# The first pass of a two-layer hybrid decoder: dot products of the conditioning, their order on two engines, and where small parameter work stands

## The chip, the cores and the metric

The kernel runs on one core of a Trainium2 chip. A core has TensorE (PE, matrix products; PEld loads its weights), VectorE (DVE), ScalarE (ACT), GpSimd (POOL) and SyncE (SP, which here issues most transfers). The metric is device time in microseconds of one execution; a lower time is better.

## What is computed

The reference is a decoder trunk of two layers on 512 tokens of width 1024, in float32. What matters here is the start of a layer:

```python
for l in range(DEPTH):
    cond = jax.nn.silu(c) @ w_ada[l] + b_ada[l]
    shift, scale, gate_raw = jnp.split(cond, 3, axis=-1)
    h = x * (1.0 + scale[:, None]) + shift[:, None]
    proj = h @ w_in[l]          # 49 column tiles of 128: HGRN2, RWKV-7, merge gates
    ...                         # two token mixers on proj, merged by sigmoid gates
    x = layer_norm(DN_ALPHA * x + (1.0 + gate_raw[:, None]) * out, ln_g[l], ln_b[l])
```

The vector `c` (1024 numbers) sets, through a dot product with each column of `w_ada`, one shift and one scale for each of the 1024 channels of `h`. Nothing of the projection can start on a slice of `h` before the shift and the scale of its 128 channels are there. `lower_bounds`, a softmax over the two layers of a small parameter, enters the forget gate of HGRN2.

## The kernel before, in words

Channels lie on the 128 partitions and tokens on the free axis, so `h` is eight slices ("columns" below, `kt` 0 to 7) of 128 channels x 512 tokens. Each product is made of three: operands are cut into a rounded part (hi) and a remainder (lo), and hi x hi, hi x lo and lo x hi are added in PSUM.

**Start.** One row of `c` is loaded (L149), a product with a row of ones (L168) spreads it over all partitions in two halves of 512, and `c_rows` (L173) makes silu of it with a tanh on ScalarE and one operation on VectorE for each half. `NWARM` = 5 products on a mask (L928) keep TensorE busy meanwhile. VectorE also prepares small parameters of both layers (L209 to L239: scaled copies, and the softmax with two exponentials on ScalarE).

**First pass** (L876 to L951). For each column `kt`, `first_load` loads 128 x 512 of `x` and two tiles of `w_ada` (128 x 1024 each, 512 KB), and `ada_col` makes the shift (`dvsh`) and the scale (`dvsc`): two half dots of 512 and an addition for each, by L309. `first_h` makes the slice of `h` on ScalarE (`u`, L124), rounds it (`A`, L122, ScalarE) and takes the remainder on VectorE (`A`, L127). Seven column tiles of `w_in` (`first`, L863) are then multiplied with the slice, so that a column gives 21 products (L949 to L951) into seven PSUM tiles, which stay open over all eight columns. The weights come in 28 pieces of 128 x 256 (`unit_loads`); `unit_splits` rounds each on ScalarE (L122) and takes its remainder on GpSimd (L127); a piece serves two columns. The table `ORD` says behind which column which load is issued: a number below 8 is the load of that column, 8 the masks, and 11, 20 and 21 the second, third and fourth seven pieces of weights.

**After it.** The seven PSUM tiles feed the heads of layer 0: `hg_f` (tanh on ScalarE, then two operations on VectorE with `dvh` and `dvlbm`, the softmax's results), `hg_q`, and so on. Head by head, the chains of the mixers are woven with further projections (L268 to L273).

**What sets the order.** The program is written as one stream; a scheduler places the instructions of each engine in an order of its own, within data dependences, buffers and what `issue_after` demands. Each engine then works strictly in its order. SyncE issues transfers in order too, and waits where the target is still being read.

Of the kernel before, what the change touches and what calls it, by code (L numbers as in the profile page):

```python
# [19 lines left out]
WAZ = (1, 1, 1, 1, 1, 1, 1, 1)  # L20
WAB = (1, 1, 1, 1, 1, 1, 1, 1, 0)
NWARM = 5
ORD = ((11, 2), (3, 20), (4,), (5, 6), (21,7), (8,), (), ())

WHZ = (0, 16, 5, 6, 7, 7, 8, 6, 4, 4)
WHS = (0, 14, 5, 6, 7, 8, 9, 8, 6, 6)
# [57 lines left out]
def body(ctx, tc, d):  # L84
    nc = tc.nc
    V, A, G, PE = nc.vector, nc.scalar, nc.gpsimd, nc.tensor
# [18 lines left out]
    def u(shape=(128, 512), dt=F32):  # L105
        return st("u", list(shape), dt)
# [10 lines left out]
    def cst(name, shape, dt=F32):  # L117
        return cp.tile(list(shape), dt, name=name)

    def act(out, in_, f, scale=1.0, bias=0.0):  # L120
        if f == AF.Copy:
            A.activation(out, in_, f, scale=scale)  # L122
# [21 lines left out]
    mm = PE.matmul  # L144
    PK = (A.copy, V.tensor_copy)


    crow = st("G", [1, 1024])
    nc.sync.dma_start(crow, d["c"].rearrange("(a k) -> a k", a=1))  # L149
    prm = cst("prm", (128, NPRM))  # L150
    nc.scalar.dma_start(prm, d["prm"])
    cc = cst("cc", (128, NCONST))
# [11 lines left out]
    ones = u((128, 128))  # L164
    G.memset(ones, 1.0)
    craw = [ps("rw"), ps("rw")]
    for h in range(2):
        cmm = mm(craw[h], ones[0:1], crow[:, h * 512:(h + 1) * 512], start=True, stop=True)  # L168
    mbd = cst("mbd", (128, 4, 128))
    silc = []  # L170

    def c_rows(craw):

        silc[:] = [mbd.rearrange("p a b -> p (a b)"), st("W", [128, 512])]
# [4 lines left out]
    c_rows(craw)  # L179
    ident = cc[:, NC_ID:NC_ID + 128]  # L180
    bonesr = cst("bonesr", (128, 128), F32R)
    for i in range(2):
# [11 lines left out]
    cs = cst("cs", (128, 8))  # L194
# [4 lines left out]
    def P(n, l, i=None, w=None):  # L199
        o = PO[n, l]  # L200
        if i is not None:
            return prm[:, o + i:o + i + 1]
        return prm[:, o:o + w]

    dv = [dict() for _ in range(L)]
    for l in range(L):
        for n, w in (("omm", 17), ("omka", 4), ("h1", 4), ("h1n", 4), ("lbm", 4), ("kkh", 4), ("sc1", 8), ("sh", 8),
                     ("ga", 8)):
            dv[l][n] = cst(f"dv{n}{l}", (128, w))  # L209
        ts(V, dv[l]["omm"], P("mu", l, w=17), -1.0, 1.0, ALU.mult, ALU.add)  # L210
        V.tensor_scalar_mul(dv[l]["kkh"], P("kk", l, w=4), -0.5)
        ts(V, dv[l]["omka"], P("ka", l, w=4), -0.5, 1.0, ALU.mult, ALU.add)

        for n in ("w0", "a0", "ka", "v0")[:4 if l else 3]:
            V.tensor_scalar_mul(P(n, l, w=4), P(n, l, w=4), 0.5)
        V.tensor_scalar_add(P("bsc", l, w=16), P("bsc", l, w=16), 1.0)


    lbm = cst("lbm", (128, 4))
    lbe = [cst(f"lbe{l}", (128, 4)) for l in range(L)]  # L220
    lb = cst("lb", (128, 4))
    lbt = cst("lbt", (128, 4))
    tt(V, lbm, P("lbr", 0, w=4), P("lbr", 1, w=4), ALU.max)
    for l in range(L):
        tt(V, lbe[l], P("lbr", l, w=4), lbm, ALU.subtract)
        act(lbe[l], lbe[l], AF.Exp)
    tt(V, lbt, lbe[0], lbe[1], ALU.add)
    V.reciprocal(lbt, lbt)
    for l in range(L):
        mul(V, lbe[l], lbe[l], lbt)  # L230
    for l in range(L):
        if l == 0:
            tt(V, lb, lbe[0], lbe[0], ALU.subtract)
        else:
            tt(V, lb, lbe[0], lbe[1], ALU.add)
            tt(V, lb, lb, lbe[0], ALU.subtract)
        ts(V, dv[l]["h1"], lb, -0.5, 0.5, ALU.mult, ALU.add)
        V.tensor_scalar_mul(dv[l]["h1n"], dv[l]["h1"], -1.0)
        V.tensor_scalar_max(dv[l]["lbm"], lb, 1e-30)  # L239


    piece = [512]

    def split(raw, hi, lo, e=None):

        act(hi, raw, AF.Copy)
        for i in range(0, raw.shape[-1], piece[0]):
            x = slice(i, min(i + piece[0], raw.shape[-1]))
            tt(e or G, lo[:, x], raw[:, x], hi[:, x].bitcast(F32), ALU.subtract)

    def wunit(src, th="wh", tl="wl"):
        raw = st("raw", [128, 512])
# [49 lines left out]
    def ada_col(l, n, k, w, run=True):  # L302

        o = dv[l][("sh", "sc1", "ga")[n]][:, k:k + 1]
        init = P(("bsh", "bsc", "bga")[n], l, k)
        part = st("sm", [128, 2])

        def half(h):
            V.tensor_tensor_reduce(out=w[h], in0=w[h], in1=silc[h], scale=0.5, scalar=0.0 if h else init, op0=ALU.mult,  # L309
                                   op1=ALU.add, accum_out=part[:, h:h + 1])  # L310
            if h:
                tt(V, o, part[:, 0:1], part[:, 1:2], ALU.add)
        if run:
# [566 lines left out]
    xin = []  # L880

    def first_load(kt):
        if kt % 2 == 0:
            xin.append(st("t4" if kt < 6 else "G", [128, 2, 512]))
        if kt:
            nc.sync.dma_start(xin[kt // 2][:, kt % 2], d["xt"][kt])
        hs = []
        for n in range(2):
            w = wada[kt % 2][:, (kt // 2 % 2 * 2 + n) * 1024:(kt // 2 % 2 * 2 + n) * 1024 + 1024]
            nc.sync.dma_start(w, d["w_ada"][0, n, kt])  # L890
            hs.append(ada_col(0, n, kt, (w[:, 0:512], w[:, 512:1024]), kt > 0))
        if kt == 0:
            nc.sync.dma_start(xin[0][:, 0], d["xt"][0])
            for f in hs:
                for h in range(2):
                    f(h)

    def first_h(kt):
        hx = u()
        sc, sh = dv[0]["sc1"][:, kt:kt + 1], dv[0]["sh"][:, kt:kt + 1]  # L900
        if kt == 0:
            ts(V, hx, xin[0][:, 0], sc, sh, ALU.mult, ALU.add)
        else:
# [97 lines left out]
    for l in range(L):  # L1001
# [409 lines left out]
```

## Time and profile before

| what | value |
|---|---|
| time, median of 3 runs | 977.59 us (976.17 to 984.16) |
| profiled execution | 974.99 us, span 973.1 us |
| PE busy | 931.4 us, 96% of the span |
| DVE busy | 736.9 us, 76% |
| POOL busy | 584.5 us, 60% |
| ACT busy | 455.8 us, 47% |
| mean granted TensorE clock | 0.99 of full speed |

The span is the time from the first to the last instruction of the profiled execution; 1.9 us lie around it. A matrix unit that is busy 96% of the span still has stretches in which it waits; the table does not tell where they lie, and stretches, waits and single instructions are read for that.

### The profile page before, as it was taken

The numbers are of one execution on the slowest core, as the hardware profiler recorded it, in microseconds if no ns is written. First come the engines' busy times: TensorE is split into PE (matmuls) and PEld (weight loads), VectorE is DVE, ScalarE is ACT, GpSimd is POOL, SyncE is SP. The second block draws the span as 40 slices with busy tenths as digits, with TensorE's granted clock in tenths as the row PEclk, the third lists the DMA queues.
The fourth block names the chain that finished last, engine by engine and source line by source line (L and its number), as shares of the span: only waits on it lengthen the run. The fifth ranks groups of instructions, "written<-read, shape, count | busy, mean of one in ns | idle before, by whom it ended". The sixth has DMA issues, their size and how long they took to land.

```text
span 973.1 us, 16762 instructions
## 1 busy us (share of the span) xinstructions
PE 931.4 (96%) x6132; PEld 753.2 (77%) x6132; DVE 736.9 (76%) x1277; ACT 455.8 (47%) x924; POOL 584.5 (60%) x568
## 2 busy tenths in 40 slices
PE   7888899999999999999999999999999999999996
PEld 3666688888877777888888778888888777778786
DVE  7878986769995667588876686767799676747777
ACT  3356455556334334543355655556633433453421
POOL 5466666566454666867546577667745466674435
PEclk9999999999998999999999999999999999999998
DMA  8815322323332231565642123222233323355422
GB/s 320 325 49 168 119 88 66 97 74 91 93 106 86 88 120 44 161 203 188 196 135 65 56 87 87 66 87 78 75 98 89 117 89 108 101 163 172 120 77 86
DMA packets 61748, 112.83 MB, mean 116 GB/s; under 512 B 6865, under 2 KB 11361, under 8 KB 61666
## 3 DMA queue, kind: packets, MB, share of 16 engines
q1 hardware_dynamic: 57778, 105.12, 34.8%
q10 hardware_dynamic: 3888, 6.64, 2.1%
q8 instruction: 48, 0.79, 0.3%
q14 instruction: 34, 0.28, 0.1%
HBM read 106.49 MB, written 5.25 MB: 115 GB/s over the span
## 4 chain that ended last, share of the span: by engine, by line
PE 61%; DVE 23%; DMA 3%; issue 2%; ACT 2%; POOL 1%; DVEq 0%; ACTq 0%; POOLq 0%
PE ppj L273 13%; PE ppj L268 13%; PE ppj L269 12%; DVE t L127 5%; DVE t L543 3%; DVE ar L546 2%; PE prw L599 2%; DVE t L535 2%; DMA raw<-in_w_br 2%; PE ppj L1211 2%; PE ppj L1212 2%; PE ppj L1210 2%; DVE u L127 1%; PE prw L618 1%; DVE hl L127 1%
## 5 line engine op out<-in xcount | busy, mean ns | idle before, releaser
L127 POOL TENSOR_TENSOR wl<-raw,wh 128x256 fp32r<-128x256 f32 (+1 forms) x321 | 349.5, 1103 | 256.8 <-ACT wh L122 136.8
L122 ACT ACTIVATE wh<-raw 128x512 fp32r<-128x512 f32 (+1 forms) x233 | 145.1, 625 | 172.7 <-PE ppj L269 103.3
L268 PE MATMUL ppj<-B,wh 128*128 128x512 f32 x432 | 173.6, 402 | 0.1
L269 PE MATMUL ppj<-B,wh 128*128 128x512 f32 x432 | 170.9, 396 | 0.0
L268 PE MATMUL ppj<-A,wh 128*128 128x512 f32 x400 | 161.8, 405 | 1.6 <-ACT wh L122 1.6
L269 PE MATMUL ppj<-A,wh 128*128 128x512 f32 x400 | 159.1, 398 | 0.0
L273 PE MATMUL ppj<-B,wl 128*128 128x512 f32 x432 | 123.7, 397 | 0.0
L273 PE MATMUL ppj<-A,wl 128*128 128x512 f32 x400 | 116.2, 402 | 0.0
L268 PEld LDWEIGHTS ppj<-B,wh 128*128 128x128 f32 x432 | 81.2, 188 | 16.8 <-ACT wh L122 0.5
L273 PEld LDWEIGHTS ppj<-B,wl 128*128 128x128 f32 x432 | 79.8, 188 | 16.8 <-POOL wl L127 0.2
L269 PEld LDWEIGHTS ppj<-B,wh 128*128 128x128 f32 x432 | 81.4, 188 | 14.7
L268 PEld LDWEIGHTS ppj<-A,wh 128*128 128x128 f32 x400 | 75.7, 189 | 18.5 <-ACT wh L122 3.1
L273 PEld LDWEIGHTS ppj<-A,wl 128*128 128x128 f32 x400 | 74.6, 190 | 15.6
L269 PEld LDWEIGHTS ppj<-A,wh 128*128 128x128 f32 x400 | 75.6, 189 | 13.4
L127 DVE TENSOR_TENSOR t<-t,t 128x144 f32<-128x144 f32 (+29 forms) x62 | 44.3, 715 | 2.1
L127 POOL TENSOR_TENSOR hl<-hl,u 128x256 f32<-128x256 f32 x40 | 32.1, 803 | 20.2 <-DVE u L787 9.6
L136 DVE SCALAR_TENSOR_TENSOR pr<-ppj,prm,pr 128x511 f32<-128x511 f32 x22 | 16.4, 748 | 29.6 <-ACT pr L124 29.6
L127 DVE TENSOR_TENSOR hl<-hl,u 128x256 f32<-128x256 f32 x64 | 32.5, 527 | 2.6 <-ACT u L805 1.3
L127 DVE TENSOR_TENSOR W<-prw,d 64x256 f32<-64x256 f32 x32 | 13.5, 422 | 20.0 <-PE prw L623 19.2
L517 ACT COPY X<-prw 64x128 f32<-64x128 f32 x64 | 16.8, 262 | 24.2 <-PE prw L513 23.5
L543 DVE TENSOR_REDUCE t<-t 128x4 f32<-128x4 f32 (+30 forms) x62 | 26.4, 425 | 2.1
L127 POOL TENSOR_TENSOR gm<-mbd,gam 64x256 f32<-64x256 f32 x24 | 18.9, 787 | 15.1 <-DVE mbd L127 12.3
(488 smaller groups left out, 1992.8 us busy)
## 6 DMA issues: line engine op xcount, KB each, us to landing
raw<-in_w_in SPq DMA_DIRECT2D x182, 256.0 KB, 2.6
B<-in_w_ada SPq DMA_DIRECT2D x16, 512.0 KB, 6.5
z<-in_w_ada SPq DMA_DIRECT2D x32, 256.0 KB, 3.1
u<-in_w_ada SPq DMA_DIRECT2D x32, 256.0 KB, 3.5
raw<-in_w_br SPq DMA_DIRECT2D x32, 256.0 KB, 2.7
raw<-in_w_out SPq DMA_DIRECT2D x32, 256.0 KB, 2.7
u<-in_x SPq DMA_DIRECT2D x8, 256.0 KB, 4.3
o<-in_w_in SPq DMA_DIRECT2D x14, 128.0 KB, 4.4
```

The lines of the kernel that those rows point to most:

```text
L122: A.activation(out, in_, f, scale=scale)
L127: return e.tensor_tensor(o, a, b, op=op)
L268: yield mm(o, w, xh, start=half == 0 and k == 0, stop=False)
L269: yield mm(o, w, xl, start=False, stop=False)
L273: yield mm(o, w, xh, start=False, stop=half == n - 1 and k == 3)
L535: V.transpose(Tin[qs].rearrange("p t s -> p s t"), ax[qs, :, cs_].rearrange("p h s -> p s h"))
L543: V.tensor_reduce(blk(R, t, [32, j]), pv, axis=AX.X, op=ALU.add)
L546: V.transpose(ax[qs, :, cs_].rearrange("p h t -> p t h"), R[qs].rearrange("p j t -> p t j"))
L599: mm(pg[h][:, p * 128:(p + 1) * 128], BK[p][hs, ch], ZR[p][hs, ch], start=p == 0, stop=p == 3)
L1210: yield mm(p2[:, q], mg[j][:, 0, o], wo[j][0][:, q], start=j == 0, stop=False)
L1211: yield mm(p2[:, q], mg[j][:, 0, o], wo[j][1][:, q], start=False, stop=False)
L1212: yield mm(p2[:, q], mg[j][:, 1, o], wo[j][0][:, q], start=False, stop=j == 7)
```

## The change

Five things change.

1. `c` is loaded in two halves onto partitions 0 and 64, and the two spreading products stand on different row groups of TensorE; silu of `c` lies in one tile of 1024 (`silc0`) instead of two of 512.
2. A shift or a scale is one dot of 1024 with the bias as its start value and the result written at once; the additions go.
3. VectorE's order in the first pass is written out (`queued`, the list `chain`): scale dot of a column, shift dot of the next, remainder of this one. ScalarE's too (`units`). GpSimd's remainders of the first weights stand behind the first scale (`shown`).
4. The small parameters, but for the biases, are prepared behind the last slice (`of_parameters`), with the two exponentials.
5. `ORD` loads column 4 ahead of the third seven pieces of weights (20).

```diff
-ORD = ((11, 2), (3, 20), (4,), (5, 6), (21,7), (8,), (), ())
+ORD = ((11, 2), (3, 4), (20,), (5, 6), (21, 7), (8,), (), ())
...
-    crow = st("G", [1, 1024])
-    nc.sync.dma_start(crow, d["c"].rearrange("(a k) -> a k", a=1))
+    crow = st("G", [128, 512])
+    for h in range(2):
+        nc.sync.dma_start(crow[64 * h:64 * h + 1], d["c"][h * 512:(h + 1) * 512].rearrange("(a k) -> a k", a=1))
...
-        cmm = mm(craw[h], ones[0:1], crow[:, h * 512:(h + 1) * 512], start=True, stop=True)
+        cmm = mm(craw[h], ones[64 * h:64 * h + 1], crow[64 * h:64 * h + 1], start=True, stop=True)
...
+    silc0 = st("G", [128, 1024])
+    c_rows(craw, [silc0[:, h * 512:(h + 1) * 512] for h in range(2)])
...
+    def of_parameters():
+        ...
+        tt(V, lbm, P("lbr", 0, w=4), P("lbr", 1, w=4), ALU.max)
+        for l in range(L):
+            tt(V, lbe[l], P("lbr", l, w=4), lbm, ALU.subtract)
+            act(lbe[l], lbe[l], AF.Exp)
+        ...
...
-            hs.append(ada_col(0, n, kt, (w[:, 0:512], w[:, 512:1024]), kt > 0))
+            ws[kt].append(w)
...
+    def queued(f, q=None):
+
+        q = chain if q is None else q
+        with ExitStack() as es:
+            if q:
+                es.enter_context(tc.issue_after(q[-1].ins))
+            q.append(f())
+
+    def first_col(kt, n):
+        w = ws[kt][n]
+        o = dv[0][("sh", "sc1")[n]][:, kt:kt + 1]
+        queued(lambda: V.tensor_tensor_reduce(out=w, in0=w, in1=silc0, scale=0.5, scalar=P(("bsh", "bsc")[n], 0, kt), op0=ALU.mult,
+                                              op1=ALU.add, accum_out=o))
 
     def first_h(kt):
+
         hx = u()
         sc, sh = dv[0]["sc1"][:, kt:kt + 1], dv[0]["sh"][:, kt:kt + 1]
+        first_col(kt, 1)
         if kt == 0:
-            ts(V, hx, xin[0][:, 0], sc, sh, ALU.mult, ALU.add)
+            queued(lambda: V.tensor_scalar(hx, xin[0][:, 0], sc, sh, op0=ALU.mult, op1=ALU.add))
         else:
-            act(hx, xin[kt // 2][:, kt % 2], AF.Identity, scale=sc, bias=sh)
-        hilo(hx, hT[kt], V)
+            queued(lambda: act(hx, xin[kt // 2][:, kt % 2], AF.Identity, scale=sc, bias=sh), units)
+        rounded = A.activation(hT[kt][:, 0], hx, AF.Copy)
+        if kt:
+            units.append(rounded)
+        low = lambda: queued(lambda: tt(V, hT[kt][:, 1], hx, hT[kt][:, 0].bitcast(F32), ALU.subtract))
+        if kt == 0:
+            low()
+        if kt < KT - 1:
+            first_col(kt + 1, 0)
+        if kt:
+            low()
+        return rounded
...
-            split(fr[i][:, w], fw[i][0][:, w], fw[i][1][:, w])
+            queued(lambda: split(fr[i][:, w], fw[i][0][:, w], fw[i][1][:, w]), units)
...
+    first_load(1)
+    first_col(0, 0)
     first_h(0)
-    unit_splits(0, 0)
-    first_load(1)
+
+    shown = G.tensor_copy(cs[:, 7:8], dv[0]["sc1"][:, 0:1])
+    with tc.issue_after(shown.ins):
+        unit_splits(0, 0)
...
-            first_h(kt + 1)
+            rounded = first_h(kt + 1)
+            if kt == 6:
+                with tc.issue_after(rounded.ins), tc.issue_after(chain[-1].ins):
+                    of_parameters()
```

On VectorE, behind the remainder of column 0 (`A_166`), the order before was the following (`B` holds the tiles of `w_ada`, `mbd` and `W` the halves of silu of `c`, `sm` the two partial sums, `dvsh` and `dvsc` shift and scale):

```order
L127 TENSOR_TENSOR A_166<-u_199,A_166 128x512
L309 ISA B_165,sm_233<-B_165,mbd,prm 128x512
...
L309 ISA B_165,sm_233<-B_165,W_77 128x512
...
L127 TENSOR_TENSOR dvsh_100<-sm_233 128x1
L309 ISA B_165,sm_238<-B_165,mbd,prm 128x512
...
L309 ISA B_165,sm_238<-B_165,W_77 128x512
...
L127 TENSOR_TENSOR dvsc_99<-sm_238 128x1
L127 TENSOR_TENSOR A_166<-u_261,A_166 128x512
```

In the change, from the same place (the left out rows, in both, read the accumulator):

```order
L127 TENSOR_TENSOR A_131<-u_160,A_131 128x512
L912 ISA B_130,dvsh_101<-B_130,G_78,prm 128x1024
...
L912 ISA B_130,dvsc_100<-B_130,G_78,prm 128x1024
...
L912 ISA B_129,dvsh_101<-B_129,G_78,prm 128x1024
...
L127 TENSOR_TENSOR A_131<-u_206,A_131 128x512
L912 ISA B_129,dvsc_100<-B_129,G_78,prm 128x1024
```

The remainder of column 1 (`A_131<-u_206`) has moved behind the shift dot of column 2, whose `w_ada` tile is `B_129`.

At the end of the first pass VectorE's order was this, from the last addition of a scale to the first operations of the heads:

```order
L127 TENSOR_TENSOR dvsc_99<-sm_477 128x1
L161 CAST hmask<-z_521 128x256 x4
L161 CAST hmask<-z_527 128x256
L127 TENSOR_TENSOR A_167<-u_555,A_167 128x512
L133 TENSOR_SCALAR u_605<-u_604,dvh_95 128x512
L133 TENSOR_SCALAR u_605<-u_605,dvlbm_97 128x512
L127 TENSOR_TENSOR u_611<-u_611,u_605 128x256
```

In the change it is this, of which eight rows behind the remainder, with 13 scaled copies of parameters, are left out, and a few more:

```order
L127 TENSOR_TENSOR A_132<-u_472,A_132 128x512
...
L127 TENSOR_TENSOR lbm<-prm 128x4
L127 TENSOR_TENSOR lbe_491<-prm,lbm 128x4
...
L127 TENSOR_TENSOR lbt<-lbe_491,lbe_492 128x4
L233 RECIPROCAL lbt<-lbt 128x4
L127 TENSOR_TENSOR lbe_491<-lbe_491,lbt 128x4
...
L127 TENSOR_TENSOR lb<-lbe_491 128x4
L133 TENSOR_SCALAR dvh_96<-lb 128x4
...
L133 TENSOR_SCALAR u_559<-u_558,dvh_96 128x512
L127 TENSOR_TENSOR lb<-lbe_491,lbe_492 128x4
L133 TENSOR_SCALAR u_559<-u_559,dvlbm_98 128x512
```

Between the last remainder and the heads' first operation (`u_559<-u_558`) there now stand 24 small operations.

On ScalarE, at the same place, the order before was this (`u_604` is the tanh of the heads' first operation, the others read PSUM tiles of the first pass too):

```order
L122 ACTIVATE wh_660<-raw_658 128x512
L122 ACTIVATE pu_714<-raw_712 128x512
L124 ACTIVATE u_604<-ppj_158 128x512
L730 COPY u_611<-prw_159 128x512
L124 ACTIVATE u_613<-ppj_157,dvomm_93 128x512
```

In the change:

```order
L122 ACTIVATE wh_614<-raw_612 128x512
L122 ACTIVATE pu_668<-raw_666 128x512
L124 ACTIVATE lbe_491<-lbe_491 128x4
L124 ACTIVATE lbe_492<-lbe_492 128x4
L124 ACTIVATE u_558<-ppj_123 128x512
L736 COPY u_565<-prw_124 128x512
```

The two exponentials (`lbe`) have come to stand between the last split of a weight and the heads' first tanh (`u_558`).

## Rows read from the trace of the kernel before

**Rows 1.** Busy time by stretch: stretch, its length, then PE to POOL, clock, DMA, GB/s.

```profile
14.30:63.20 48.90, 41.95 (x169) 32.05 (x170) 38.87 (x86) 21.49 (x47) 27.58 (x30) 0.97 0.66 236
63.20:134.00 70.80, 60.30 (x335) 48.74 (x334) 66.69 (x139) 40.53 (x97) 47.44 (x55) 0.98 0.39 122
134.00:973.00 839.00, 818.18 (x5618) 668.32 (x5616) 622.28 (x1011) 388.60 (x770) 504.35 (x467) 0.99 0.35 105
```

**Rows 2.** Timeline of PE: start, length, instruction, in brackets idle before and its releaser.

```profile
2.55 3.75 PE L168 MATMUL prw<-G,u 1*128 1x512 f32 x4 [2.55 <-DMA G<-in_c]
6.22 7.33 PE L928 MATMUL phg<-mask 128*128 128x512 f32 x10
14.31 0.73 PE L949 MATMUL ppj<-A,wh 128*128 128x512 f32 x2 [0.76 <-ACT A L122]
22.57 1.22 PE L949 MATMUL ppj<-A,wh 128*128 128x512 f32 x2 [3.21 <-ACT A L122]
58.29 0.73 PE L949 MATMUL ppj<-A,X 128*128 128x512 f32 x2 [0.86 <-ACT A L122]
62.96 0.39 PE L951 MATMUL phg<-A,bkt 128*128 128x512 f32 x1
63.18 0.39 PE L268 MATMUL ppj<-A,wh 128*128 128x512 f32 x1
```

**Rows 3.** Who waited for whom to 85 us: total, times, longest.

```profile
ACT u L124 <- DVE dvsc L127: 24.3, 6, 4.8
```

**Rows 4.** Timeline of DVE: first dot, one beside GpSimd's work, two alone; 256 wide.

```profile
7.64 0.75 DVE L309 CUSTOM_DVE_ANT_0 B<-B,mbd,prm 128x512 f32<-128x512 f32 x1
23.27 1.22 DVE L309 CUSTOM_DVE_ANT_0 B<-B,mbd,prm 128x512 f32<-128x512 f32 x1
42.54 0.75 DVE L309 CUSTOM_DVE_ANT_0 B<-B,mbd,prm 128x512 f32<-128x512 f32 x1
43.21 0.69 DVE L309 CUSTOM_DVE_ANT_0 B<-B,W 128x512 f32<-128x512 f32 x1
81.82 0.41 DVE L127 TENSOR_TENSOR hl<-hl,u 128x256 f32<-128x256 f32 x1
```

**Rows 5.** Timeline of POOL: a remainder beside dots, then the work at the pass's end.

```profile
23.90 1.18 POOL L127 TENSOR_TENSOR pr<-o,hl 128x256 fp32r<-128x256 f32 x1
58.84 2.83 POOL L127 TENSOR_TENSOR wl<-raw,wh 128x256 fp32r<-128x256 f32 x4 [4.34 <-ACT wh L122]
```

**Rows 6.** Timeline of PE: products on 64 rows in two groups, and on 128.

```profile
309.94 1.16 PE L599 MATMUL prw<-B,B 64*128 64x128 f32 x16
311.83 0.60 PE L611 MATMUL prw<-cc,W 128*128 128x128 f32 x4
```

**Rows 7.** Busy time by stretch, for transfers: the last figure is GB/s.

```profile
0.00:10.00 10.00, 7.45 (x9) 2.87 (x10) 5.21 (x27) 4.53 (x10) 3.66 (x15) 1.00 0.82 288
10.00:14.00 4.00, 3.55 (x7) 1.19 (x5) 3.87 (x18) 0.38 (x1) 1.47 (x3) 1.00 1.04 374
14.00:16.80 2.80, 2.49 (x11) 2.08 (x12) 2.51 (x4) 2.10 (x7) 2.16 (x3) 1.00 0.99 318
```

**Rows 8.** Timeline at the pass's end and of small work, on DVE and ACT.

```profile
3.46 0.38 DVE L215 TENSOR_SCALAR prm<-prm 128x4 f32<-128x4 f32 x4
58.27 0.69 DVE L127 TENSOR_TENSOR A<-u,A 128x512 fp32r<-128x512 f32 x1 [0.54 <-ACT A L122]
60.44 0.60 ACT L124 ACTIVATE u<-ppj 128x512 f32<-128x512 f32 x1 [0.63 <-PE ppj L951]
61.07 0.88 DVE L133 TENSOR_SCALAR u<-u,dvh 128x512 f32<-128x512 f32 x1 [2.11 <-ACT u L124]
```

**Rows 9.** One line's instructions: count, ns shortest/median/longest, first and last start.

```profile
L461 DVE TENSOR_SCALAR d<-d x8: 168/583/1008, 99.6 to 691.0; 128x8 f32<-128x8 f32 x8
```

**Rows 10.** Chain of waits in order of time: two waits of VectorE for transfers.

```profile
84.41 3.47 DMA z<-in_w_ada
...
107.88 2.55 DMA z<-in_w_ada
```

More of the change, by code (lines that the diff above doesn't have):

```diff
@@ L121, in act @@
         if f == AF.Copy:
-            A.activation(out, in_, f, scale=scale)
+            return A.activation(out, in_, f, scale=scale)
         else:
@@ L167, in body, with c_rows @@
     for h in range(2):
-        cmm = mm(craw[h], ones[0:1], crow[:, h * 512:(h + 1) * 512], start=True, stop=True)
+        cmm = mm(craw[h], ones[64 * h:64 * h + 1], crow[64 * h:64 * h + 1], start=True, stop=True)
     mbd = cst("mbd", (128, 4, 128))
     silc = []
-    def c_rows(craw):
-        silc[:] = [mbd.rearrange("p a b -> p (a b)"), st("W", [128, 512])]
+    def c_rows(craw, dst):
+        silc[:] = dst
         for h in range(2):
@@ L177, in c_rows @@
             stt(silc[h], silc[h], 1.0, craw[h], ALU.add, ALU.mult)
-    c_rows(craw)
+    silc0 = st("G", [128, 1024])
+    c_rows(craw, [silc0[:, h * 512:(h + 1) * 512] for h in range(2)])
     ident = cc[:, NC_ID:NC_ID + 128]
@@ L209, in body @@
             dv[l][n] = cst(f"dv{n}{l}", (128, w))
[L210 to L215, printed above, removed]
-        V.tensor_scalar_add(P("bsc", l, w=16), P("bsc", l, w=16), 1.0)
-    lbm = cst("lbm", (128, 4))
@@ L220, in body @@
[L220 to L239, printed above, removed]
+        V.tensor_scalar_add(P("bsc", l, w=16), P("bsc", l, w=16), 1.0)
@@ new lines, in of_parameters @@
+    def of_parameters():
+        for l in range(L):
+            ts(V, dv[l]["omm"], P("mu", l, w=17), -1.0, 1.0, ALU.mult, ALU.add)
+            V.tensor_scalar_mul(dv[l]["kkh"], P("kk", l, w=4), -0.5)
+            ts(V, dv[l]["omka"], P("ka", l, w=4), -0.5, 1.0, ALU.mult, ALU.add)
+            for n in ("w0", "a0", "ka", "v0")[:4 if l else 3]:
+                V.tensor_scalar_mul(P(n, l, w=4), P(n, l, w=4), 0.5)
+        lbm = cst("lbm", (128, 4))
+        lbe = [cst(f"lbe{l}", (128, 4)) for l in range(L)]
+        lb = cst("lb", (128, 4))
+        lbt = cst("lbt", (128, 4))
+        tt(V, lbm, P("lbr", 0, w=4), P("lbr", 1, w=4), ALU.max)
+        for l in range(L):
+            tt(V, lbe[l], P("lbr", l, w=4), lbm, ALU.subtract)
+            act(lbe[l], lbe[l], AF.Exp)
+        tt(V, lbt, lbe[0], lbe[1], ALU.add)
+        V.reciprocal(lbt, lbt)
+        for l in range(L):
+            mul(V, lbe[l], lbe[l], lbt)
+        for l in range(L):
+            if l == 0:
+                tt(V, lb, lbe[0], lbe[0], ALU.subtract)
+            else:
+                tt(V, lb, lbe[0], lbe[1], ALU.add)
+                tt(V, lb, lb, lbe[0], ALU.subtract)
+            ts(V, dv[l]["h1"], lb, -0.5, 0.5, ALU.mult, ALU.add)
+            V.tensor_scalar_mul(dv[l]["h1n"], dv[l]["h1"], -1.0)
+            V.tensor_scalar_max(dv[l]["lbm"], lb, 1e-30)
@@ L242, in body @@
     piece = [512]
     def split(raw, hi, lo, e=None):
-        act(hi, raw, AF.Copy)
+        rounded = act(hi, raw, AF.Copy)
         for i in range(0, raw.shape[-1], piece[0]):
@@ L879, in body @@
     hT = [hb[kt // 4][:, kt % 4] for kt in range(KT)]
-    xin = []
+    xin, ws, chain, units = [], {}, [], []
     def first_load(kt):
@@ L886, in first_load @@
             nc.sync.dma_start(xin[kt // 2][:, kt % 2], d["xt"][kt])
-        hs = []
+        ws[kt] = []
         for n in range(2):
@@ L890, in first_load @@
             nc.sync.dma_start(w, d["w_ada"][0, n, kt])
-            hs.append(ada_col(0, n, kt, (w[:, 0:512], w[:, 512:1024]), kt > 0))
+            ws[kt].append(w)
         if kt == 0:
             nc.sync.dma_start(xin[0][:, 0], d["xt"][0])
-            for f in hs:
-                for h in range(2):
-                    f(h)
+    def queued(f, q=None):
[9 more added lines that the diff above has]
+                                              op1=ALU.add, accum_out=o))
     def first_h(kt):
@@ L900, in first_h @@
         sc, sh = dv[0]["sc1"][:, kt:kt + 1], dv[0]["sh"][:, kt:kt + 1]
+        first_col(kt, 1)
         if kt == 0:
-            ts(V, hx, xin[0][:, 0], sc, sh, ALU.mult, ALU.add)
+            queued(lambda: V.tensor_scalar(hx, xin[0][:, 0], sc, sh, op0=ALU.mult, op1=ALU.add))
         else:
-            act(hx, xin[kt // 2][:, kt % 2], AF.Identity, scale=sc, bias=sh)
-        hilo(hx, hT[kt], V)
+            queued(lambda: act(hx, xin[kt // 2][:, kt % 2], AF.Identity, scale=sc, bias=sh), units)
[9 more added lines that the diff above has]
+            low()
+        return rounded
     def unit_loads(half, q):
@@ L1176, in body @@
                 nc.sync.dma_start(craw[h], d["c"][h * 512:(h + 1) * 512].partition_broadcast(128))
-            c_rows(craw)
+            c_rows(craw, [mbd.rearrange("p a b -> p (a b)"), st("W", [128, 512])])
             ada_next(*itertools.islice(ada, WAB[0]))
```

## The prediction

> **What bounds the kernel now.** I read the busy time by stretch first. From 134 us to the end PE is busy 818 of 839 us; from 63 to 134 us VectorE leads with 66.7 of 70.8; in the first pass, 14.3 to 63.2, no engine is full: PE 42.0 of 48.9, VectorE 38.9 [rows 1]. So a gain at the front moves all the rest forward, provided that it reaches VectorE's chain in the heads. Then PE's timeline: the first real product stands at 14.31, and the first one behind the pass (L268) at 63.18 [rows 2]. Products follow each other at some 0.227 us (62.96 to 63.18; the last column's 21 take 4.89 with a slow first pair), so 8 columns x 21 make 38.1 us, and 48.9 - 38.1 = 10.8 us of the pass is waiting. The waits say for what: the slice of `h` waits on ScalarE for the scale of VectorE, 24.3 us in six waits, up to 4.8 [rows 3].
>
> Why the scale is late is read in rows of VectorE and GpSimd. A half dot alone steps at 0.67 us (42.54 to 43.21); beside GpSimd's remainders it takes 1.22, and a remainder then takes 1.18 against 0.69 undisturbed (four in 2.83) [rows 4, 5]. The two take turns of 1.15 us in all, some 0.59 of it GpSimd's and 0.56 VectorE's.
>
> **The change part by part**, against the profiled execution, 974.99 us (the median shown, 977.59, is 2.6 above it).
>
> *Start.* Products on 64 rows of two groups run two at a time: 16 passes take 1.16 us, where 4 on 128 rows take 0.60 [rows 6]. The spreading of `c` takes 3.75 us in four passes [rows 2]; in pairs it takes half, less some 0.4 because the second half of `c` is a second transfer: VectorE's first dot comes about 1.1 us earlier, at 6.5 instead of 7.64 [rows 4] (bounds: 0, if the groups don't overlap here, and 1.5). Parameters no longer stand between the dots. Two dots of 1.2 each, the slice and its rounding at 0.6 each (operations of 512 take 0.60 to 0.69 [rows 8]) put the first slice at 10.1. But PE is then still warming up: that work takes 7.33 us and begins where the spreading ends [rows 2], so it ends near 12.3. Start gained: 2 us, of which nothing is kept, as the next step shows.
>
> *Column 1.* In VectorE's new order the remainder of column 1 stands behind the shift dot of column 2, and that dot needs its 512 KB. By then 5.24 MB have been asked for: 2.1 of `w_ada` for columns 0 and 1, 0.52 for the dot, 0.79 of `x`, 14 pieces of 0.131. The transfers bring 2.88 MB to 10 us, 1.50 to 14 and 0.89 to 16.8 [rows 7], 5.27 in all, so the tile lands near 16.8. Dot, one turn of GpSimd and remainder (1.12 + 0.59 + 0.57, and often a second turn) put the remainder at 19.4. PE has finished column 0 at 12.3 + 4.8 = 17.1 and waits 2.3 us: its second product of column 1 needs the remainder. This is a new wait, on VectorE behind a transfer; before, column 1 began at 22.57 [rows 2].
>
> *Columns 1 to 7.* From there PE needs 21 x 0.227 = 4.77 us a column. VectorE and GpSimd need, taking turns: a dot of 1024 is a half dot's turn and another 512 (0.69 for an operation of 512, 0.41 for one of 256 [rows 4, 8], so 0.56 more), 1.12; two of them, a remainder of 0.57 and 3.5 remainders of GpSimd at 0.59 make 4.88. The wider dot saves no turn time; what goes is the additions, and the order by which ScalarE's slice stood behind splits. With both near 4.8, column 7 begins at 19.4 + 6 x 4.8 = 48.2, and the first product behind the pass comes at 53.0 instead of 63.18: 10.2 us. Lower bound 50.4, with no wait at column 1 (12.3 + 38.1); upper 56, if a dot's turn is 20% longer (6 columns x 2 x 0.22, and a late last remainder). The load of column 4 now stands ahead of the pieces 20, four of which go to buffers that GpSimd's remainders of the pieces 11 still read, so that SyncE waits there. Behind that wait stands the load of column 5. GpSimd's seven remainders of the pieces 11 take up to 1.7 us each beside wide dots and end near 26; that load then lands near 31, when VectorE asks for it. I cost it at nothing, and at 1 us if GpSimd is later.
>
> *Parameters behind the last slice.* This is the largest new cost. Before, VectorE was idle for 2.11 us there and began the heads at 61.07, right behind the tanh of 60.44 [rows 8]. Now 24 small operations stand in that place, and the two exponentials stand ahead of that tanh on ScalarE. Alone, 13 scaled copies at 0.075 (four take 0.38 with their end), three operations, the exponentials and six that hang on each other take about 2.6 us and would be just covered. But GpSimd works there, four remainders from 58.84 and two more behind them [rows 5], and small operations wait for its turns too: one on 8 numbers takes 168 ns at best, 583 in the median [rows 9]. About five of the six remainders fall behind the last slice: five turns of 0.67 with one small operation each, 3.4 us, then eleven operations in 1.0, the exponentials and their way to and from ScalarE 0.5 (an estimate: three small operations), and six dependent ones 0.8: 5.7 us behind the last remainder, which ends near 48.3. The heads begin at 54.0 instead of 61.07: 7.1 us. With no turns (lower bound of the cost) they begin at 50.9; if all six remainders fall behind and the six dependent ones take 583 ns each, at 57.
>
> *Behind it.* The heads' first two operations, 0.88 us the first [rows 8], no longer meet GpSimd (some 0.3 less each), seven more small operations stand among the first (+0.5), which about cancels. From there on the orders agree but for places in the heads of layer 0. Sum: 974.99 - 7.2 = 967.8, and with the 2.6 between the profiled run and the median, **970.4 us**.
>
> **The rivals.**
> - *The parameters slip through.* The small operations find the turns free, or GpSimd's six remainders are done by then. For it: ScalarE rounds those weights in a row, right behind the last slice, and PE ends the pass 4.8 us later in any case. Then 10.2 to 12 us are kept: 966.5 (965 to 968).
> - *PE loses its clock.* A wait of 3.21 us ahead of column 1 was followed by two products in 1.22 us instead of 0.73 [rows 2], half the clock for some 7 products, 1.4 us. If the new wait of 2.3 us does that too, and a weight's remainder comes late besides: 972.5.
> - *The heads give it back.* VectorE waits 3.47 and 2.55 us for gate columns there [rows 10], and one weight load now stands ahead of such a pair in SyncE's order. If these waits grow by half: 973.5.
> - *Slower: the wide dot streams at half pace.* Its turn would be 2.24 us, a column 2 x 2.24 + 0.57 + 2.07 = 7.1; from the first slice at 12.5 the last remainder ends at 62, the heads begin near 68: 984.5. It decides from a turn of 1.8 us, where the heads begin at 61 again. Against it: a half dot with the same two float32 operands steps at 0.67 us, near one column in a nanosecond [rows 4]. [...]
>
> **How the numbers follow.** Forecast, 970.4 (968 to 973): 0.42. Parameters slip through: 0.30. Clock: 0.14. Heads: 0.11. Slower: 0.03. About 1% (9.8 us) is what a measurement of this kernel tells from no change; faster by that means under 967.8, most of the second case and the edge of the first: 0.33. Slower by 1%: 0.03, the rest 0.64. The range of 965 to 975.5 leaves out the slow case and the ends of the others, below 2 in 10.
>
> **What would show it.** Right: the first dot near 6.5; first slice near 10.1, but first product at 12 or later; column 1 held by VectorE's remainder behind a transfer; columns then 4.8 us apart; the first product behind the pass near 53; VectorE's `dvh` some 5.7 us behind the last remainder, with small operations of 0.5 us and more. Wrong: columns over 5.3 us apart (the turns), small operations all near 0.16 us (no turns), or a shift of the heads' begin that is not found again at the end.

## The result, and the profile after

The change runs in 961.51 us (median of 4: 960.64 to 965.81), the kernel before on the same chip in 979.54 (median of 4: 976.17 to 984.16): ratio 0.984, 95% interval 0.981 to 0.987. It is faster by 1.6%. 970.4 us was predicted, with a range from 965 to 975.5, so the prediction is wrong: 8.9 us more came than its sum gives. The profiled execution took 961.35 us (span 959.4), 13.6 less than the one before. The stretches that answer to [rows 1], with the same columns:

```profile
11.30:57.06 45.76, 42.21 (x171) 33.67 (x169) 40.00 (x72) 21.77 (x46) 39.47 (x34) 0.93 0.82 290
57.06:127.50 70.44, 62.07 (x332) 50.32 (x331) 67.39 (x139) 39.98 (x96) 43.22 (x52) 0.93 0.38 116
127.50:959.40 831.90, 814.25 (x5622) 666.08 (x5620) 619.50 (x1010) 387.96 (x771) 502.69 (x466) 1.00 0.35 106
```

The first pass is 3.1 us shorter (45.76 for 48.9) and begins 3.0 us earlier; the heads take what they took. But the last stretch is 7 us shorter too, though the engines have the same instructions there as before (but for one clearing of `mbd`, 0.52 us of GpSimd, which now stands at the start). That is what the prediction did not have.

The front in PE's timeline, against [rows 2]:

```profile
2.17 2.55 PE L170 MATMUL prw<-G,u 1*128 1x512 f32 x4 [2.17 <-POOL mask L196]
4.65 7.21 PE L957 MATMUL phg<-mask 128*128 128x512 f32 x10
11.30 1.03 PE L985 MATMUL ppj<-A,wh 128*128 128x512 f32 x2
17.68 0.50 PE L985 MATMUL ppj<-A,wh 128*128 128x512 f32 x1 [0.43 <-ACT A L924]
21.00 0.79 PE L986 MATMUL ppj<-A,wh 128*128 128x512 f32 x1 [2.83 <-DVE A L127]
22.02 0.63 PE L985 MATMUL ppj<-A,wh 128*128 128x512 f32 x1
57.06 0.39 PE L274 MATMUL ppj<-A,wh 128*128 128x512 f32 x1
```

PE waits 2.83 us at column 1 for VectorE's remainder. Products then take 0.63 instead of 0.39 us: the granted clock is half from 20.3 to 27.1 us. After that no wait of PE stands in the pass, and the first product behind it comes at 57.06. VectorE's timeline of the same stretch, with the waits and the small operations ([rows 4, 8] before):

```profile
6.20 1.28 DVE L912 CUSTOM_DVE_ANT_0 B<-B,G,prm 128x1024 f32<-128x1024 f32 x1
18.40 1.42 DVE L912 CUSTOM_DVE_ANT_0 B<-B,G,prm 128x1024 f32<-128x1024 f32 x1 [2.29 <-DMA B<-in_w_ada]
19.75 1.20 DVE L127 TENSOR_TENSOR A<-u,A 128x512 fp32r<-128x512 f32 x1
20.87 1.75 DVE L912 CUSTOM_DVE_ANT_0 B<-B,G,prm 128x1024 f32<-128x1024 f32 x1
48.01 0.68 DVE L127 TENSOR_TENSOR A<-u,A 128x512 fp32r<-128x512 f32 x1
48.61 0.71 DVE L133 TENSOR_SCALAR dvomm<-prm 128x17 f32<-128x17 f32 x1
49.24 0.16 DVE L218 TENSOR_SCALAR dvkkh<-prm 128x4 f32<-128x4 f32 x1
54.66 0.48 DVE L133 TENSOR_SCALAR u<-u,dvh 128x512 f32<-128x512 f32 x1
```

The heads begin at 54.66 instead of 61.07. ScalarE's row shows that two things end there together: the tanh they need waited for PE and ends at 54.46.

```profile
53.86 0.60 ACT L124 ACTIVATE u<-ppj 128x512 f32<-128x512 f32 x1 [0.32 <-PE ppj L987]
```

**Where the rest came from.** The same instruction, found in both traces, tells by its two start times how far the change is ahead:

| instruction | before | change | ahead |
|---|---|---|---|
| heads' first operation, VectorE | 61.07 | 54.66 | 6.4 |
| first transpose of the inversion of layer 0 | 230.32 | 223.75 | 6.57 |
| first product on `X,G` behind it (L623, L629) | 304.01 | 292.13 | 11.9 |
| first transpose of the inversion of layer 1 | 696.80 | 684.55 | 12.2 |
| second product on `t` behind it (L572, L578) | 758.30 | 744.67 | 13.6 |
| end of the span | 973.1 | 959.4 | 13.7 |

So 6.6 us are of the front; 5.3 arise at the inversion of layer 0 and 1.4 at that of layer 1. In the inversion (`rw_invert`, a triangular inverse of all heads) VectorE transposes the tile `ar` into working tiles, does 31 multiplications and 31 sums, and transposes back, while PE multiplies on. VectorE's groups there, before (230.3 to 290.4) and in the change (223.7 to 281.5); columns: operation, count, busy time, mean ns, idle:

```profile
L127 DVE TENSOR_TENSOR t<-t,t 128x144 f32<-128x144 f32 (+29 forms) x31 | 22.2, 715 | 1.1
...
L546 DVE STREAM_TRANSPOSE ar<-t 32x1024 f32<-32x1024 f32 x4 | 9.3, 2333 | 0.1
L535 DVE STREAM_TRANSPOSE t<-ar 32x1024 f32<-32x1024 f32 x4 | 9.0, 2247 | 0.1
L549 DVE STREAM_TRANSPOSE t<-t 32x1024 f32<-32x1024 f32 x2 | 4.1, 2048 | 0.0
```

```profile
L127 DVE TENSOR_TENSOR t<-t,t 128x144 f32<-128x144 f32 (+29 forms) x31 | 21.4, 690 | 1.1
...
L541 DVE STREAM_TRANSPOSE t<-ar 32x1024 f32<-32x1024 f32 x4 | 8.4, 2095 | 0.1
L552 DVE STREAM_TRANSPOSE ar<-t 32x1024 f32<-32x1024 f32 x4 | 8.4, 2090 | 0.1
L555 DVE STREAM_TRANSPOSE t<-t 32x1024 f32<-32x1024 f32 x2 | 4.1, 2046 | 0.0
```

The eight transposes that touch `ar` take 1.5 us less, the two that do not take the same; the multiplications fall by another 0.8 (from 22.2 to 21.4). One that meets a remainder of GpSimd is longer: that of 128x36 takes 0.96 us before, at 240.20, where a remainder runs from 239.79 to 241.11, and 0.20 in the change, at 233.02, where none runs. From first to last transpose it is 60.07 us before and 57.73 in the change, 60.01 and 57.66 in layer 1. What these 2.3 us are worth is seen in the stretches behind it, before and then in the change (columns of [rows 1]):

```profile
290.00:294.00 4.00, 2.16 (x38) 1.35 (x36) 3.46 (x5) 0.00 (x0) 0.75 (x1) 1.00 0.37 109
294.00:302.00 8.00, 8.00 (x125) 6.39 (x123) 4.28 (x7) 4.32 (x7) 2.95 (x2) 0.57 0.12 34
```

```profile
281.00:285.00 4.00, 4.00 (x47) 3.13 (x46) 3.42 (x6) 1.36 (x3) 1.50 (x2) 1.00 0.62 200
285.00:291.00 6.00, 6.00 (x128) 4.78 (x127) 4.24 (x6) 3.68 (x6) 1.99 (x2) 1.00 0.26 64
```

Before, PE stands still for 1.84 us in front of the products that need the inverse, and its clock is then half from 295.1 to 302.0 (0.57 in the mean of the second stretch), which costs another 3.4: half of those 6.9 us. In the change VectorE is just in time, PE never stops, and the clock stays.

### The profile page after: what moved, and what is told of

Its sections match the earlier page's. It is cut to its first block, busy times and chain, and to the rows that moved or that the text cites. A ratio compares the mean times of both kernels' runs of the same rounds, so it can differ in the third digit from the quotient of the medians.

```text
span 959.4 us, 16715 instructions
## 1 busy us (share of the span) xinstructions
PE 927.7 (97%) x6132; PEld 753.9 (79%) x6132; DVE 732.2 (76%) x1229; ACT 455.3 (47%) x924; POOL 589.6 (61%) x569
## 4 chain that ended last, share of the span: by engine, by line
PE 79%; DVE 11%; DMA 4%; ACT 2%; issue 2%; POOL 1%; SPq 0%; DVEq 0%; ACTq 0%; POOLq 0%
PE ppj L279 17%; PE ppj L274 17%; PE ppj L275 16%; PE prw L605 2%; DMA raw<-in_w_br 2%; PE ppj L1247 1%; PE ppj L1248 1%; DMA raw<-in_w_in 1%; PE ppj L1246 1%; PE prw L624 1%; DVE u L127 1%; PE prw L629 1%; PE prw L642 1%; DVE z L315 1%; DVE hl L127 1%
## 5 line engine op out<-in xcount | busy, mean ns | idle before, releaser
L127 POOL TENSOR_TENSOR wl<-raw,wh 128x256 fp32r<-128x256 f32 (+1 forms) x321 | 344.1, 1086 | 244.8 <-ACT wh L122 128.8
L912 DVE CUSTOM_DVE_ANT_0 B<-B,G,prm 128x1024 f32<-128x1024 f32 x16 | 26.0, 1647 | 6.0 <-DMA B<-in_w_ada 5.9
L127 POOL TENSOR_TENSOR gm<-mbd,gam 64x256 f32<-64x256 f32 x24 | 18.9, 787 | 15.4 <-DVE mbd L127 12.3
```

Of the source, the lines that this page charges most:

```text
L912: queued(lambda: V.tensor_tensor_reduce(out=w, in0=w, in1=silc0, scale=0.5, scalar=P(("bsh", "bsc")[n], 0, kt), op0=ALU.mult, op1=ALU.add, ...
```

## The experiments

Each kernel ran beside the kernel before; medians of 4 to 10 runs. How far two medians differ by chance is seen in the first: one kernel, twice on the same chip, gave 977.52 and 980.26 us. Single traces differ too. Five kernels (the change, 5, 7, 8 and 14) have the same order of instructions on every engine; in their traces PE waits 2.83 to 4.19 us at column 1, the heads begin between 54.66 and 55.95, and the first transpose of layer 0 between 222.18 and 225.20.

**1. The kernel before, unchanged.** Is the late gain an accident of one execution?

> The kernel before, unchanged, with a second profile. In its first profile PE waited 1.83 us ahead of the products behind the inversion of layer 0 (near 291 us), and its clock then stood at half from 295.1 to 302.0; the change has neither, and 5.3 of the 13.6 us between the two profiles arise there. Theory turns by luck: VectorE and GpSimd take turns in the inversion, and the outcome differs from execution to execution of one kernel; this profile then shows the wait with even odds, and without it the span is near 968 us. Theory set by the program: the wait is there again (1.5 to 2.2 us, half clock behind it), span 972 to 980. Time 975 to 983 us either way, since the runs so far lay there.

977.52 us (973.09 to 985.15). The inversions take 61.17 and 60.03 us, PE waits 1.1 us for the first (1.5 to 2.2 were expected), and its clock is again half, from 284.8 for 3.4 us. So the late loss is there again and belongs to the kernel; its size differs from execution to execution.

**2. The change with the parameters at the start.**

```diff
-            if kt == 6:
-                with tc.issue_after(rounded.ins), tc.issue_after(chain[-1].ins):
-                    of_parameters()
+    of_parameters()          # behind its definition
```

> The change, with the small parameters prepared at the start, as before. Prediction's own reading: they cost 5.7 us behind the last remainder, so the heads would begin up to 5 us earlier than 54.66 and the time fall to about 957. Rival, from the profile of the change: PE ends the first pass only at 57, the tanh that waits for it ends at 54.46, and the parameters cost 0.2 us; heads at 54.4 to 55.5 (the start 0 to 1 us later), time 961 to 963.

971.15 us (966.31 to 971.96): neither. The heads begin at 53.91, as the rival said, yet 9.6 us are lost. The inversions take 60.04 and 60.00, and PE's wait and half clock behind them are back.

**3. The remainder of column 1 ahead of the shift dot of column 2.**

```diff
-        if kt == 0:
+        if kt < 2:
             low()
         if kt < KT - 1:
             first_col(kt + 1, 0)
-        if kt:
+        if kt > 1:
             low()
```

> The change, with VectorE's remainder of column 1 ahead of the shift dot of column 2 (one place in the order). Both theories: PE's wait of 2.83 us at column 1 falls to under 0.7. If that wait is also what put the clock at half from 20.3 to 27.1, this goes too, and PE ends the pass near 52 to 54 instead of 57.06. Theory parameters next: the heads still begin near 54.5, held by the 24 small operations now, and the time stays within 0.5 us of the change's 961.5. Rival, PE alone sets the heads: they begin 3 to 5 us earlier, time 957 to 958.5.

961.03 us (960.40 to 962.14), the change's time. PE's wait at column 1 is 0.21 us and no half clock stands in the pass. PE's and VectorE's timelines of this kernel:

```profile
17.79 0.50 PE L986 MATMUL ppj<-A,wh 128*128 128x512 f32 x1 [0.21 <-DVE A L127]
53.26 0.50 PE L274 MATMUL ppj<-A,wh 128*128 128x512 f32 x1
```

```profile
47.19 0.68 DVE L127 TENSOR_TENSOR A<-u,A 128x512 fp32r<-128x512 f32 x1
53.84 0.48 DVE L133 TENSOR_SCALAR u<-u,dvh 128x512 f32<-128x512 f32 x1
```

PE leaves the pass 3.8 us earlier, but the heads begin only 0.8 earlier: now the small operations, 6 us behind the last remainder, hold them. The heads' begin is not the whole story, though. At the first transpose of layer 0 this kernel is 2.7 us ahead of the change (221.06 for 223.75), at that of layer 1 only 0.1 (684.45 for 684.55): what PE gained passes through the heads and is lost between the layers, from 395 to 435 us.

**4. Both edits.**

> Both edits: parameters at the start and the remainder of column 1 ahead of the shift dot of column 2. If each of them covers for the other, the heads begin 2.5 to 4 us earlier than with either alone (near 51.5; VectorE's last remainder at 48.7 is then the bound), time 957.5 to 959.5. If VectorE's transfers set the end of the pass, nothing is gained: 961 to 962.

971.94 us (969.21 to 974.48). The heads begin at 51.63, 3.0 us earlier, where each edit alone gave 0.8: each did cover for the other, at this place. At the first transpose of layer 0 (221.52) nothing is left of it against the third kernel (221.06). The time misses by 13 us, with inversions of 60.05 and 60.01. So every kernel that *creates* the parameters' tiles at the start is slow there, whatever its order. As built, the five small tiles (`lbm`, two `lbe`, `lb`, `lbt`, each 32 bytes of a partition) then lie ahead of `ar` and push it from byte 26144 to 26304.

**5 to 8. The place alone.** In these four each engine's instructions and their order are the same as in the kernel that they come from; only the place in memory of `ar` and some small tiles differs. Of each edit only the new lines are shown; the tiles' old lines go.

```diff
 # 5: the change, the five tiles created ahead of ar, used where the change uses them
+    lbm = cst("lbm", (128, 4))
+    lbe = [cst(f"lbe{l}", (128, 4)) for l in range(L)]
+    lb = cst("lb", (128, 4))
+    lbt = cst("lbt", (128, 4))
     def of_parameters():
 # 6: the kernel before, one line moved up
+    ar = cst("ar", (128, 2, 4, 4, 64))
     lbm = cst("lbm", (128, 4))
 # 7: the change, lbm alone ahead of ar;   8: lbm and lbt
```

> The change with the five small tiles of the parameters (lbm, two lbe, lb, lbt) created where they were created before, their work left where the change puts it: every engine's order is that of the change, but the tile ar and five smaller tiles behind it lie 160 bytes higher in each partition, as in the kernel before. Theory place: the inversion (first to last transpose) takes 60.0 us in both layers instead of 57.7, PE waits about 1.8 us for it in layer 0 and falls to half clock, time 967 to 971. Theory program: it was not the place but the order of work at the start; inversions 57.7, time 960 to 963.

> The kernel before with the tile ar created ahead of the five small tiles: ar lies 160 bytes lower, at the place it has in the change, the five behind it, everything else at its old place, every engine's order unchanged. Theory place: inversions 57.7 us instead of 60.0, no wait ahead of the products behind them and no half clock at 285 to 302, time 969 to 973. If it is another tile than ar that matters, or the program: inversions 60.0, time 976 to 982.

> The change with only lbm created ahead of ar: ar 32 bytes higher than in the change, at a multiple of 64 bytes, as it was before. If a multiple of 64 is what costs: inversions 60.0, time 967 to 971. If it is the distance to other tiles: in between or as the change, 960 to 965.

> The change with lbm and lbt created ahead of ar: ar 64 bytes higher than in the change, as in the change 32 above a multiple of 64. If a multiple of 64 is what costs: inversions 57.7, time 960 to 963. If every step upward costs: 967 to 971.

Results: 972.07 (965.25 to 974.11), 970.24 (968.16 to 971.36), 968.21 (966.69 to 972.20) and 963.32 (959.68 to 965.52). Theory place holds in all four by the inversion of layer 0 (60.06, 57.73, 60.02 and 57.72 us), with the fifth's time 1 us over what it gave and the eighth's 0.3; and a place of `ar` at a multiple of 64 bytes is what the slow ones share (26304 and 26176, against 26144 and 26208). The multiplications go with the place too, though they do not touch `ar`: 22.2 us in the fifth kernel, 21.4 in the sixth. The sixth kernel, which only moves a line, is 1.1% faster than the kernel before (ratio 0.989, 0.985 to 0.993). Its groups and stretches at the same places as before:

```profile
L535 DVE STREAM_TRANSPOSE t<-ar 32x1024 f32<-32x1024 f32 x4 | 8.4, 2104 | 0.1
L546 DVE STREAM_TRANSPOSE ar<-t 32x1024 f32<-32x1024 f32 x4 | 8.4, 2088 | 0.1
```

```profile
290.00:294.00 4.00, 4.00 (x136) 3.12 (x135) 3.24 (x5) 0.92 (x2) 0.68 (x1) 1.00 0.30 99
294.00:302.00 8.00, 8.00 (x74) 5.99 (x73) 5.65 (x10) 4.78 (x9) 4.35 (x4) 1.00 0.31 101
```

The fifth, with the change's order, shows the signs of before:

```profile
L553 DVE STREAM_TRANSPOSE ar<-t 32x1024 f32<-32x1024 f32 x4 | 9.3, 2320 | 0.1
L542 DVE STREAM_TRANSPOSE t<-ar 32x1024 f32<-32x1024 f32 x4 | 9.0, 2242 | 0.1
```

```profile
281.00:285.00 4.00, 2.16 (x12) 1.39 (x11) 3.88 (x4) 0.43 (x1) 1.29 (x1) 1.00 0.60 188
285.00:293.00 8.00, 8.00 (x149) 6.32 (x149) 4.82 (x5) 3.68 (x6) 1.57 (x2) 0.58 0.02 6
```

**9 and 10. Both edits, and the parameters at the start alone, with `ar` created first.**

```diff
+    ar = cst("ar", (128, 2, 4, 4, 64))
     of_parameters()
```

> Parameters at the start and the remainder of column 1 ahead of the shift dot of column 2, as in the fourth kernel, with ar created ahead of the five small tiles, at the place it has in the change. Theory place: what that kernel lost behind 280 us against the change, 7 to 8 us, comes back: inversions 57.7, time 960 to 962.5; the heads again begin near 51.6, 3 us earlier than in the change. Theory that parameters at the start harm something else later: 966 or more.

> The change with the parameters prepared at the start, and ar created ahead of the five small tiles. Theory place: the 10 us that the second kernel lost come back but for what the start costs: time 961 to 963.5, heads near 53.9. Rival, small work at the start costs by itself: 966 to 971.

960.94 (959.36 to 962.10) and 963.07 us (962.35 to 966.50): the 11 and 8 us that the fourth and second kernels lost are back. Heads' begin and time, all four with `ar` at byte 26144:

| | remainder of column 1 behind the dot | ahead of it |
|---|---|---|
| parameters behind the last slice | 54.66, 961.51 us | 53.84, 961.03 us |
| parameters at the start | 54.10, 963.07 us | 51.96, 960.94 us |

The ninth is the best version found, by no more than the runs scatter. Of its 2.7 us at the heads 2.55 are still there at the inversion (221.20 for 223.75). At the border of the layers VectorE's chain gives 1.8 of them back. One piece of that: a dot there takes 1.81 us in the ninth kernel (second row) and 0.74 in the change (first row), where GpSimd stands still from 400.68 to 402.17.

```profile
401.15 0.74 DVE L315 CUSTOM_DVE_ANT_0 z<-z,mbd,prm 128x512 f32<-128x512 f32 x1
```

```profile
399.33 1.81 DVE L317 CUSTOM_DVE_ANT_0 z<-z,mbd,prm 128x512 f32<-128x512 f32 x1
```

**11. The old order of loads.**

```diff
-ORD = ((11, 2), (3, 4), (20,), (5, 6), (21, 7), (8,), (), ())
+ORD = ((11, 2), (3, 20), (4,), (5, 6), (21,7), (8,), (), ())
```

> The change with the old table of loads: the third seven pieces of weights ahead of column 4. The prediction cost this part at nothing: time within 1 us of the change, 960.5 to 963. Rival, the loads of columns are what VectorE waits for in the second half (0.32 and 1.39 us in the change): column 4 later by 0.9 MB of pieces, 2 to 3 us, heads 1 to 3 us later, time 962.5 to 965.

964.80 us (962.68 to 967.11), heads at 57.76, 1.8 to 3.1 later than in the five kernels with the change's order: the rival's mechanism. VectorE waits for columns where the change waits 0.32 and 1.39 us:

```profile
30.97 1.29 DVE L912 CUSTOM_DVE_ANT_0 B<-B,G,prm 128x1024 f32<-128x1024 f32 x1 [2.48 <-DMA B<-in_w_ada]
44.88 1.82 DVE L912 CUSTOM_DVE_ANT_0 B<-B,G,prm 128x1024 f32<-128x1024 f32 x1 [2.64 <-DMA B<-in_w_ada]
```

What that is worth at the end is not shown: the first transpose of layer 0 stands at 225.17, within the range of the five kernels, and the eighth and the fourteenth, whose inversions are fast like the change's, took 963.32 and 966.11 us.

**12. `c` in one row, on one row group.**

```diff
-    crow = st("G", [128, 512])
+    crow = st("G", [1, 1024])
...
-        cmm = mm(craw[h], ones[64 * h:64 * h + 1], crow[64 * h:64 * h + 1], start=True, stop=True)
+        cmm = mm(craw[h], ones[0:1], crow[:, h * 512:(h + 1) * 512], start=True, stop=True)
```

> The change with c loaded in one row and spread by products on one row group, as before. The first dot then stands near 7.4 instead of 6.20, and PE's warm-up, which begins behind the spreading, ends 1.2 us later, near 12.3. Prediction's reading: nothing is kept of this, because column 1 waits for the transfer that lands near 18.4 either way: heads within 0.5 us of 54.66, time 960.5 to 963. Rival, the start moves everything: heads 1.2 us later, time 962.5 to 963.5.

First dot at 7.46, heads at 55.13 (0.5 later, within the range of the five kernels with the change's order), time 965.01, but its six runs lie between 960.61 and 967.38. So the 1.26 us at the first dot are not found again at the heads; what they are worth at the end is not told by these runs. One thing differs: PE waits 2.63 us at column 1 here too, yet no half clock follows in the pass, and the first product behind the pass comes at 54.56.

**13 and 14. The other operands moved.** The last constant tile is 32 bytes longer, so that all working tiles move and `ar` stays.

```diff
-cst("bs4", (128, 4, 6))
+cst("bs4", (128, 32))[:, 0:24].rearrange("p (a b) -> p a b", b=6)
```

> The kernel before with the last constant tile made 32 bytes longer: ar stays at its place, a multiple of 64 bytes, and the pool of all working tiles behind it (among them the other operands of the inversion) moves 32 bytes up, from multiples of 64 to 32 above. Orders unchanged. If the inversion is slow because ar and its partners stand alike within 64 bytes: 57.7 us now, time 968 to 972. If a place of ar at a multiple of 64 is slow by itself: 60.0, time 975 to 983. Every other operation between working tiles keeps its relation, so neither theory expects a difference elsewhere.

> The change with the same 32 bytes: ar stays 32 above a multiple of 64, the working tiles move there too. If standing alike is what is slow: inversions 60.0, time 967 to 973. If ar's own place decides: 57.7, time 960 to 966.

The kernel before so moved takes 970.95 us (968.18 to 976.35) with inversions of 57.66 and 57.64; the change 966.11 (963.32 to 967.83) with 57.68 and 57.63. The transposes of the thirteenth, then of the fourteenth:

```profile
L535 DVE STREAM_TRANSPOSE t<-ar 32x1024 f32<-32x1024 f32 x4 | 8.4, 2095 | 0.1
L546 DVE STREAM_TRANSPOSE ar<-t 32x1024 f32<-32x1024 f32 x4 | 8.3, 2082 | 0.1
```

```profile
L541 DVE STREAM_TRANSPOSE t<-ar 32x1024 f32<-32x1024 f32 x4 | 8.4, 2094 | 0.1
L552 DVE STREAM_TRANSPOSE ar<-t 32x1024 f32<-32x1024 f32 x4 | 8.4, 2088 | 0.1
```

Neither theory as it was put: only `ar` and its partners both at multiples of 64 bytes is slow.

| `ar` modulo 64 | working tiles modulo 64 | inversions, us | kernels |
|---|---|---|---|
| 0 | 0 | 60.0 (once each 61.2 and 61.1) | before (twice), 2, 4, 5, 7 |
| 32 | 0 | 57.7 | change, 3, 6, 8 to 12 |
| 0 | 32 | 57.7 | 13 |
| 32 | 32 | 57.7 | 14 |

The half clock behind the inversion of layer 0 stands in all six traces of the first line and in none of the other ten.

Why, the runs don't tell, and the table allows a second reading. In the six slow traces `ar` and the working tiles all begin 64 bytes above a multiple of 128, so that they lie a whole multiple of 128 bytes apart. In the fourteenth they stand alike within 64 bytes but not within 128 (32 and 96). So standing alike within 128 bytes fits all sixteen traces as well as multiples of 64 do; no run tells the two apart. Nor is such a place enough by itself: the transposes between two working tiles, which also stand alike within 128 bytes and (but for 13 and 14) at multiples of 64, take 2.05 us everywhere.

That the fourteenth is 4.6 us behind the change is not the inversion. Its trace shows a wait of 4.2 us at column 1, which the seventh kernel has too (4.19), and later losses; what made them was not tried.

## Why the prediction was wrong, point by point

**The step that failed is "Behind it"**, where the sum took the rest as unchanged because "the orders agree". They do agree; the durations don't. By creating five tiles later, the fourth part of the change moved `ar` by 160 bytes, and the inversions became 2.3 us shorter each. That was worth 5 to 11 us in the medians: 979.1 against 970.2 in the order of before, 972.1 against 961.5 and 968.2 against 963.3 in that of the change. With `ar` at the old place, the change takes 972.07 (965.25 to 974.11): the forecast of 970.4 was a forecast of that kernel. Of the 8.9 us that it missed, 6.7 arise at the inversions (5.3 and 1.4) and 2.4 are of the median (the last point below); the front gave 0.6 less than the 7.2 of the sum, and 0.3 more came elsewhere.

**The sum of the front held, partly by luck.** Predicted 7.1 at the heads, measured 6.4. VectorE's chain came as forecast (heads at 54.66 for 54.0), but PE left the pass 4 us later than forecast (57.06 for 53.0). That this did not show at the heads is luck: the small parameters end 0.2 us behind the tanh that waited for PE.
- *Start.* First dot 6.20 (6.5 predicted), first product 11.30 (12 or later). The twelfth kernel confirms the term: one row group puts the dot at 7.46.
- *Column 1.* The mechanism stood: VectorE's remainder behind a transfer, 2.83 us of waiting (2.3). The tile landed near 18.4 instead of 16.8.
- *Clock.* What the rival with 0.14 feared came true, though not its 972.5 us. With the clock at half, 14 products took some 0.43 us instead of 0.227, and the pass ended at 57.06. Without it and the wait, in the third kernel, it ended at 53.26. That this is near the forecast's 53.0 is luck: the 53.0 hold a wait of 2.3 us, and without it the prediction's figure was 50.4. The third kernel starts earlier than that figure assumes (11.27 for 12.3), but PE still stands idle for 2.2 of the 42.3 us from 11.00 to 53.26, and first products behind short waits are slow (0.50 us instead of 0.39 behind its waits of 0.21, 0.43, 0.74 and 0.79 us).
- *Parameters.* Between the end of the last remainder (48.69) and the heads lie 5.97 us; 5.7 were predicted, with the turns of 0.7 that the prediction named (the small operation at 48.61 takes 0.71 us, that at 49.24 takes 0.16). But PE was late too, and the tanh ended at 54.46, so they cost 0.2 to 0.6 here, and 1.9 (53.84 against 51.96) once PE was not late. At the first transpose of layer 0 even that is gone (221.06 against 221.20).
- *Load order.* Costed at nothing. Without it VectorE waits 2.5 and 2.6 us for columns and the heads begin at 57.76, 1.8 to 3.1 us later than with it; what it is worth at the end is not shown.
- *Wide dots.* They step at 1.21 us alone (6.20 to 7.41) and at 1.68 beside GpSimd (20.87 to 22.55); two with a remainder make a column of 4.5 us where no transfer is late (remainders at 24.22 and 28.71), under the 4.88 predicted. So the rival of half pace did not come: no run shows its turn of 2.24 us, and the steps of 1.21 and 1.68 us stand in its place.
- *Heads.* The rival in which they give the gain back did not come: from their first operation to the inversion it is 169.1 us, 169.3 before.
- *Median.* The 2.6 us added for the runs of before were not found: the change's profiled run lies at its median.

## What to carry to other kernels

When two programs have the same instructions in the same order over a long stretch and differ in time there, compare the durations group by group: an operation that is longer by some 10% on one tile, and equal on others, points to where that tile lies (here a transpose took 2.25 and 2.33 us instead of 2.09 where it touched `ar`, and 2.05 in both kernels where it did not). Moving the creation of a tile is a change in itself; look at what it displaces before crediting the order of work. A late engine of 2 us costs PE more than 2 us where the wait is followed by a stretch at half clock (before, behind the inversion of layer 0: 1.84 us of waiting, and another 3.4). Two causes that end together hide each other: undo them singly and together, and follow the gain past the place where they meet, since here it was lost between the layers. And before a difference of 1 us in one trace is read, see how far traces of the same order differ.

## What the runs showed of the hardware that was not expected

- A transpose of 32 x 1024 on VectorE between `ar` and a working tile takes 2.09 us in the mean, and 2.24 to 2.33 where both tiles begin at a multiple of 64 bytes, the same in all six traces with that layout and in none of the other ten. In all six the two tiles also lie a whole multiple of 128 bytes apart, and no run separates that from the 64. Transposes between two working tiles, which stand alike too, take 2.05 us and do not show it.
- PE's waits of 1.8 us (before, behind the inversion) and 2.8 us (change, column 1) each came with 6.8 us at half clock, a loss of 3.4 and some 2.8 us on top of the wait. The wait alone does not tell the loss: 2.82 us at the same column in the tenth kernel came with 3.4 us at half clock, 2.63 us in the twelfth with none.
